# Unread matmuls in the pauses of a hand-ordered beginning, a later load of constants, and products moved ahead

## The chip, the cores and the metric

The kernel runs on one core of a Trainium2 chip. The metric is the time of the device for one execution, in microseconds (us), as the median of several runs. Beside these runs one execution is recorded by the hardware profiler: its span, from the first to the last instruction, and every instruction in it. The core's engines work side by side, each through its own instructions in order: TensorE (PE: matmuls; PEld: the loads of its stationary operand), VectorE (DVE), ScalarE (ACT), GpSimd (POOL) and SyncE (SP), which issues most DMA transfers here.

## The reference

A trunk of four residual layers over 256 tokens of 1024 features. Each layer has a token mixer (layer 0 and 3: sliding-window attention; 1: gated linear attention; 2: forgetting attention) and a SwiGLU network, each behind a norm that is shifted and scaled by vectors from the conditioning vector c. What matters for the change is the beginning of layer 0:

```
c_act = silu(c)
mod = c_act @ ada_w[0] + ada_b[0]              # 6 vectors of 1024
sh1, sc1, g1, sh2, sc2, g2 = split(mod, 6)
h = rmsnorm(x, gain) * (1 + sc1) + sh1
q, k, v = split(h @ w_in, ...)                 # 1024, 256 and 256 columns
q, k = rope(q), rope(k)                        # rotation by the position
...                                            # windowed softmax attention, output product
```

## The kernel before, in words

**Layout.** x is kept transposed: 8 tiles (KT) of 128 features by 256 tokens (S). Weights stream from memory in blocks of 1 MB, 128 partitions by 2048 columns of float32, which SP loads into one of five buffers `raw` (class `Stream`; a new load is issued when the block five before it is used up). A block of an ordinary weight is split into a high part `wh` (ACT, L195, a rounded copy) and a low part `wl` (DVE, L197, the rest), in two pieces of 1024 columns. There are three `wh`/`wl` pairs. Each product of float32 accuracy is then three matmuls of the faster format (`mm3`, L280 to L282): wh by hh, wl by hh, wh by hl, where hh and hl are the two parts of the activation h.

**The beginning** (`first_chunks`). Three kinds of blocks alternate in the stream, in the order of `ORDER0`: s and h are blocks of the scale and the shift vector of the first norm, w are blocks ("chunks") of the input projection. Chunk 0 holds the columns of the keys, chunk 1 those of the values; the next four give the queries.

1. ACT squares the 8 tiles of x, DVE adds the squares up, TensorE sums them over the partitions (`stat_start` L329, `stat_end` L342), ACT and DVE make 1/rms of it (`y`), TensorE spreads it over the partitions (L352), ACT copies it (`rbs`).
2. Four rounds follow. Round r uses one block s and one block h, which give two tiles each of scale and shift. A block is multiplied by c_act on TensorE (`ada_rows`, 16 matmul records at L231, "row products"), ACT copies the row that results (`fc`, L232), TensorE turns it into columns (L236, "turns": 4 records for a block, 8 for the two blocks of a round), and DVE adds the bias (L238). `h_tiles` then makes two tiles of h: DVE tk (L455), ACT hh (L457), DVE hl (L450). Between its two blocks a round does the products of chunk 0 with the tiles of the round before (`products`: 12 matmuls for two tiles). Behind rounds 0 and 2 the weights of chunk 0 and chunk 1 are split.
3. After the four rounds come the products that are left: chunk 1 with tiles 0 to 5, then both chunks with tiles 6 and 7.

`pinned` ties the instructions of `first_chunks` together, on each engine, in the order in which they are written. Everything else is put in order by the framework's scheduler, which may place other instructions between them.

**The second constants** (`const2`, 128 by 1024 of float32, 512 KB: the cosines and sines of the rotation, the masks of attention and more) are loaded by a DMA on ACT's queue, which stands behind round 1 in `first_chunks` (L809). The profile gives their tile and their source the same names as the first constants (const, in_const). The first to read them is the rotation of the keys (`rope`, L676 to L685, on DVE), which follows when chunk 0 is complete; then come the rotations of the queries (L676 to L683). TensorE turns the rotated keys (L701) and queries (L716) for attention, whose steps run beside the projections.

Of the kernel before, what the change touches and what calls it, by code (L numbers as in the profile page):

```python
# [20 lines left out]
S = 256  # L21
# [122 lines left out]
class Builder:  # L144
# [578 lines left out]
    def swa_heads(self, layer, pool, q_of, kT, v, oh, ol):  # L723
# [7 lines left out]
        def head(h):  # L731
            g, i = divmod(h, 4)
            rows = slice((i % 2) * HD, (i % 2 + 1) * HD)

            def pre():
                q = q_of(g)
                if g not in qTs and q is not None:
                    qTs[g] = self.swa_qT(pool, q)
                return q is not None
            return {  # L740
                "pre": pre, "ready": lambda: True,
                "q": lambda: qTs[g][rows, i // 2],
                "k": lambda: kT[0][rows, g],
                "v": lambda: [v[:, b, g * HD:(g + 1) * HD] for b in range(NB)],
                "sink": nsink[:, h:h + 1],
            }
        return self.attn_heads(pool, [head(h) for h in range(16)], self.c("masks")[:, :2 * P], oh, ol)

    def pinned(self, start):

        last = {}
        for ins in list(self.nc.cur_bb.bb.instructions)[start:]:
            if ins.engine in last:
                self.tc.add_manual_dep(
                    ins, last[ins.engine].name,
                    mybir.DependencyInfo(mybir.DependencyClass.NoSync, mybir.DependencyReason.DATA),
                    reason="first chunks")
            last[ins.engine] = ins

    def first_chunks(self):  # L760


        nc = self.nc
        start = len(nc.cur_bb.bb.instructions)
        self.A, self.late = None, []
        self.st.cap = self.st.widx[EARLY]
        self.per_tick = 0.0
        self.turns = []
        acc = None
        for k in range(KT):  # L770
            q = self.t(self.small, [P, S], "sq", bufs=4)
            nc.scalar.activation(q, self.x[:, k], AF.Square)
            if 0 < k < KT - 1:
                nc.vector.tensor_tensor(out=q, in0=acc, in1=q, op=ALU.add)
            acc, self.acc = q, acc
        self.last_sq = acc
        self.stat_start(self.acc)
        self.stat_end()
        rbs = self.t(self.small, [P, S], "rbs", bufs=1)
        nc.scalar.copy(rbs, self.spread(self.y))  # L780
        hs = hh, hl = self.h_alloc()
        A = self.t(self.small, [P, KT], "A", bufs=2)
        sh = self.mod[0][:, :KT]
        outs, ws, todo = [], [], []

        def products(n, chunks=slice(None)):
            for c, (wh, wl) in list(enumerate(ws))[chunks]:
                for k in range(todo[c], n):
                    for m in range(2):
                        sl = slice(m * P, (m + 1) * P)  # L790
                        self.mm3(outs[c][m][:, :S], hh[:, k, sl], hl[:, k, sl], wh[:, k], wl[:, k],
                                 k == 0, k == KT - 1)
                todo[c] = n
        for r in range(4):
            self.st.force_ada(0, (1,), r)
            products(2 * r, slice(1))
            self.st.force_ada(0, (0,), r)
            while self.turns:
                self.turns.pop(0)()
            self.mod_cols(0, 0, 2 * r, 2 * r + 2, A)  # L800
            self.h_tiles(range(2 * r, 2 * r + 2), rbs, A, sh, hh, hl)
            if r in (0, 2):
                c = len(ws)
                ws.append([x.rearrange("p (k n) -> p k n", k=KT) for x in self.st.get(f"i0_{c}")])
                self.st.cap = self.st.widx[EARLY]
                outs.append(self.banks(("mm", "s")[c])[0])
                todo.append(0)
            if r == 1:
                nc.scalar.dma_start(self.const2, self.a["const2"])  # L809
        products(KT - 2)  # L810
        products(KT)
        self.pinned(start)
        return hs, [[o[:, :S] for o in out] for out in outs]
# [649 lines left out]
```

## Time and profile before

| | |
|---|---|
| time, median of 3 runs | 1241.97 us (1241.35 to 1245.2) |
| time of the profiled execution | 1240.14 us |
| its span | 1238.4 us |
| mean granted TensorE clock | 0.997 |
| busy: PE, DVE, ACT, POOL | 97%, 80%, 57%, 10% of the span |
| DMA | 298.40 MB, mean 241 GB/s |

The profiled execution's time is its span and 1.7 us around it. Line numbers are those of the kernel before. In the profile, "mm" and "s" are the PSUM banks of chunk 0 and of chunk 1 in the beginning, "t" those of the row products, the turns and the sums. A float32 matmul of full accuracy shows as two records. In a list of waits or a timeline, "<-" behind the idle time names what ended it.

### The profile page before, as it was taken

The numbers are of one execution on the slowest core, as the hardware profiler recorded it, in microseconds if no ns is written. First come the engines' busy times: TensorE is split into PE (matmuls) and PEld (weight loads), VectorE is DVE, ScalarE is ACT, GpSimd is POOL, SyncE is SP. The second block draws the span as 40 slices with busy tenths as digits, with TensorE's granted clock in tenths as the row PEclk, the third lists the DMA queues.
The fourth block names the chain that finished last, engine by engine and source line by source line (L and its number), as shares of the span: only waits on it lengthen the run. The fifth ranks groups of instructions, "written<-read, shape, count | busy, mean of one in ns | idle before, by whom it ended". The sixth has DMA issues, their size and how long they took to land.

```text
span 1238.4 us, 19970 instructions
## 1 busy us (share of the span) xinstructions
PE 1207.4 (97%) x7540; PEld 1050.9 (85%) x7540; DVE 993.3 (80%) x1832; ACT 700.2 (57%) x1297; POOL 124.7 (10%) x173
## 2 busy tenths in 40 slices
PE   6999999999999999999999999999999999999997
PEld 4876988888988998888889999888889979888886
DVE  3888998889868799888877758988887998766553
ACT  4575744454676565444458777544445677544442
POOL 0020300001123111000121102100011011100011
PEclk9999999999999999999999999999999999999999
DMA  9956699889642248997875543889787534656440
GB/s 365 366 183 261 227 369 344 315 315 355 228 148 103 103 141 314 351 332 259 282 294 205 198 144 118 330 333 340 258 284 274 179 134 166 238 208 217 160 164 34
DMA packets 45106, 298.40 MB, mean 241 GB/s; under 512 B 5217, under 2 KB 5377, under 8 KB 14802
## 3 DMA queue, kind: packets, MB, share of 16 engines
q1 hardware_dynamic: 44210, 295.56, 65.6%
q8 instruction: 59, 0.97, 0.3%
q10 hardware_dynamic: 432, 1.05, 0.2%
q0 software_dynamic: 368, 0.53, 0.1%
q14 instruction: 37, 0.30, 0.1%
HBM read 296.03 MB, written 1.05 MB: 240 GB/s over the span
## 4 chain that ended last, share of the span: by engine, by line
PE 88%; DVE 5%; ACT 4%; issue 2%; POOL 0%; DMA 0%; DVEq 0%; SPq 0%; ACTq 0%; POOLq 0%
PE mm L1194 13%; PE mm L280 12%; PE mm L281 12%; PE mm L282 12%; PE s L282 7%; PE s L280 7%; PE s L281 7%; PE mm L1196 7%; PE s L613 2%; PE o L643 2%; PE t L1166 1%; PE t L654 1%; DVE wl L197 1%; ACT wh L195 1%; DVE x L551 1%
## 5 line engine op out<-in xcount | busy, mean ns | idle before, releaser
L197 DVE TENSOR_TENSOR wl<-raw,wh 128x1024 fp32r<-128x1024 f32 (+2 forms) x408 | 446.6, 1125 | 87.2 <-ACT wh L195 86.3
L195 ACT CAST wh<-raw 128x1024 fp32r<-128x1024 f32 (+2 forms) x408 | 376.8, 964 | 216.8 <-issue 91.7
L1194 PE MATMUL mm<-a,wh 128*128 128x512 f32 x704 | 247.9, 394 | 0.0
L214 DVE CUSTOM_DVE_ANT_0 raw<-raw,cact,const 128x1024 f32<-128x1024 f32 x168 | 214.1, 1290 | 4.7 <-DMA raw<-in_ada 4.5
L280 PE MATMUL mm<-wh,hh 128*128 128x512 f32 (+1 forms) x560 | 197.6, 353 | 2.0 <-ACT wh L195 1.1
L1196 PE MATMUL mm<-a,wl 128*128 128x256 f32 x704 | 196.6, 279 | 0.0
L281 PE MATMUL mm<-wl,hh 128*128 128x512 f32 (+1 forms) x560 | 193.4, 345 | 0.9 <-DVE wl L197 0.9
L282 PE MATMUL mm<-wh,hl 128*128 128x512 f32 (+1 forms) x560 | 193.8, 346 | 0.0
L1194 PEld LDWEIGHTS mm<-a,wh 128*128 128x128 f32 x704 | 131.9, 187 | 31.0
L280 PE MATMUL s<-wh,hh 128*128 128x512 f32 (+2 forms) x384 | 144.8, 378 | 1.5 <-ACT hh L457 1.5
L281 PE MATMUL s<-wl,hh 128*128 128x512 f32 (+2 forms) x384 | 142.6, 372 | 0.0
L282 PE MATMUL s<-wh,hl 128*128 128x512 f32 (+2 forms) x384 | 142.3, 374 | 0.0
L1196 PEld LDWEIGHTS mm<-a,wl 128*128 128x128 f32 x704 | 132.0, 187 | 0.2
L436 POOL TENSOR_TENSOR sq<-sq,sq 128x256 f32<-128x256 f32 x48 | 52.2, 1088 | 771.1 <-ACT sq L425 751.5
L280 PEld LDWEIGHTS mm<-wh,hh 128*128 128x128 f32 x560 | 106.1, 189 | 18.7 <-issue 3.5
L281 PEld LDWEIGHTS mm<-wl,hh 128*128 128x128 f32 x560 | 106.1, 190 | 13.9 <-DVE wl L197 1.1
L282 PEld LDWEIGHTS mm<-wh,hl 128*128 128x128 f32 x560 | 106.0, 189 | 13.8 <-issue 0.5
L551 DVE SCALAR_TENSOR_TENSOR x<-mm,mod,x 128x256 f32<-128x256 f32 x128 | 61.4, 479 | 40.2 <-PE mm L1196 32.2
L280 PEld LDWEIGHTS s<-wh,hh 128*128 128x128 f32 x384 | 72.2, 188 | 13.6 <-ACT hh L457 1.7
L282 PEld LDWEIGHTS s<-wh,hl 128*128 128x128 f32 x384 | 71.7, 188 | 13.3 <-DVE hl L450 0.2
L281 PEld LDWEIGHTS s<-wl,hh 128*128 128x128 f32 x384 | 72.3, 188 | 12.0
L280 PE MATMUL mm<-oh,wh 128*128 128x256 f32 x256 | 73.5, 292 | 1.7 <-DVE x L551 1.6
(228 smaller groups left out, 2009.5 us busy)
## 6 DMA issues: line engine op xcount, KB each, us to landing
raw<-in_ada SPq DMA_DIRECT2D x96, 1024.0 KB, 6.6
raw<-in_gu SPq DMA_DIRECT2D x88, 1024.0 KB, 6.5
raw<-in_down SPq DMA_DIRECT2D x64, 704.0 KB, 5.3
raw<-in_swa_in SPq DMA_DIRECT2D x12, 1024.0 KB, 5.9
raw<-in_gla_in SPq DMA_DIRECT2D x11, 1024.0 KB, 5.3
raw<-in_fox_in SPq DMA_DIRECT2D x11, 1024.0 KB, 4.9
raw<-in_swa_o SPq DMA_DIRECT2D x8, 1024.0 KB, 4.9
raw<-in_gla_o SPq DMA_DIRECT2D x4, 1024.0 KB, 4.9
```

Source lines behind the costliest of these rows:

```text
L195: nc.scalar.copy(wh[:, sl], raw[:, sl])
L197: eng.tensor_tensor(out=wl[:, sl], in0=raw[:, sl], in1=wh[:, sl].bitcast(F32), op=ALU.subtract)
L214: nc.vector.tensor_tensor_reduce(out=w, in0=w, in1=self.cact, scale=1.0, scalar=b, op0=ALU.mult, op1=ALU.add, accum_out=col)
L280: nc.tensor.matmul(out, ah, bh, start=first, stop=False)
L281: nc.tensor.matmul(out, ah, bl, start=False, stop=False)
L282: nc.tensor.matmul(out, al, bh, start=False, stop=last)
L436: (eng or nc.gpsimd).tensor_tensor(out=q, in0=self.acc, in1=q, op=ALU.add)
L551: self.nc.vector.scalar_tensor_tensor(out=self.x[:, m], in0=ps, scalar=gate[:, m:m + 1], in1=self.x[:, m], op0=ALU.mult, op1=ALU.add)
L613: nc.tensor.matmul(sc[:, so:s1], q[:, so:so + P], k[:, :k1], start=True, stop=True)
L643: nc.tensor.matmul(o[rows, b * P:S], vs[e][b], pt[:, e, :S] if b == 0 else pt[:, e, S:], start=b == 0, stop=b == 1)
L1194: nc.tensor.matmul(o, wh[:, k], a[:, kk].rearrange("p e n -> p (e n)"), start=kk == 0, stop=False)
L1196: nc.tensor.matmul(o[:, S:], wl[:, k], a[:, kk, 0], start=False, stop=kk == FT - 1)
```

## The change

- A new helper, `fill(n)`, issues n float32 matmuls of the identity with 256 columns of the first constants into a spare PSUM bank (tag "o", which attention's output uses later). Nobody reads their result. They are part of the pinned order of TensorE.
- Five of them stand ahead of the norm's sums, one behind the sums, one in each round between the second row product and the turns, and four, two and two at the end of rounds 0, 1 and 2, behind the issue of `h_tiles`.
- In round 3, chunk 1's products with tiles 0 to 3 (24 matmuls) stand ahead of the second row product. They were behind the turns. `todo` keeps the larger count, so that chunk 0 isn't done twice.
- The load of the second constants moves from the end of round 1 to the end of round 3.

```diff
+    def fill(self, n):
+        ident = self.c("ident")
+        for _ in range(n):
+            self.nc.tensor.matmul(self.spare[:, :S], ident, self.const[:, :S], start=True, stop=True)
...
         acc = None
+        self.spare = self.ps("o")
         for k in range(KT):
...
         self.last_sq = acc
+        self.fill(5)
         self.stat_start(self.acc)
         self.stat_end()
+        self.fill(1)
         rbs = self.t(self.small, [P, S], "rbs", bufs=1)
...
-                todo[c] = n
+                todo[c] = max(todo[c], n)
         for r in range(4):
             self.st.force_ada(0, (1,), r)
             products(2 * r, slice(1))
+            if r == 3:
+                products(4)
             self.st.force_ada(0, (0,), r)
+            self.fill(1)
             while self.turns:
                 self.turns.pop(0)()
             self.mod_cols(0, 0, 2 * r, 2 * r + 2, A)
             self.h_tiles(range(2 * r, 2 * r + 2), rbs, A, sh, hh, hl)
...
-            if r == 1:
+            if r < 3:
+                self.fill((4, 2, 2)[r])
+            else:
                 nc.scalar.dma_start(self.const2, self.a["const2"])
         products(KT - 2)
         products(KT)
```

## The prediction

> **What bounds the kernel now.** I read the page's busy shares and its chain first; then the table by stage (from:to, length, busy time of TensorE, its weight loads, DVE, ACT and POOL, granted clock, DMA share, GB/s), for the whole span and for the first 45 us; last the timelines of the first 60 us (start, length, engine, line, out<-in, and in brackets the idle time before with what ended it).
>
> ```profile
> span 1238.4 us, 19970 instructions
> PE 1207.4 (97%) x7540; PEld 1050.9 (85%) x7540; DVE 993.3 (80%) x1832; ACT 700.2 (57%) x1297; POOL 124.7 (10%) x173
> PE 88%; DVE 5%; ACT 4%; issue 2%; POOL 0%; DMA 0%; DVEq 0%; SPq 0%; ACTq 0%; POOLq 0%
> ...
> 0.00:31.00 31.00, 21.12 (x152) 12.81 (x152) 11.07 (x28) 12.99 (x26) 1.43 (x9) 0.94 0.92 364
> 155.00:186.00 31.00, 31.00 (x144) 25.53 (x143) 31.00 (x46) 13.76 (x19) 0.00 (x0) 1.00 0.98 370
> ```
>
> TensorE is busy in 97% of the span and carries 88% of the chain. A stage of the middle (last row) has no gap in it; the first 31 us have ten. So a microsecond that TensorE saves or loses in the beginning moves the end by about as much, and little else in the change can move it. The beginning has little to give: 0.3% of this kernel, about what a measurement of it can tell from no change, is 3.7 us.
>
> TensorE's timeline, and behind it four rows of the table by stage:
>
> ```profile
> 3.40 3.77 PE L1326 MATMUL mm<-hh,fc 1*128 1x512 f32 x4 [3.40 <-ACT hh L1321]
> 10.04 1.01 PE L329 MATMUL t<-const,sq 128*128 128x1 f32 x4 [2.86 <-DVE sq L774]
> 10.92 0.99 PE L342 MATMUL t<-const,sq 128*128 128x1 f32 x4
> 12.46 1.22 PE L352 MATMUL t<-const,y 128*128 128x128 f32 x4 [0.55 <-DVE y L346]
> 13.61 3.06 PE L231 MATMUL t<-raw,ccol 128*32 128x256 f32 x32
> 16.61 1.18 PE L236 MATMUL t<-const,fc 128*128 128x1 f32 x8
> 18.44 1.07 PE L231 MATMUL t<-raw,ccol 128*32 128x256 f32 x16 [0.66 <-DMA raw<-in_ada]
> 20.57 0.39 PE L280 MATMUL mm<-wh,hh 128*128 128x256 f32 x1 [1.06 <-ACT wh L195]
> 21.83 0.39 PE L281 MATMUL mm<-wl,hh 128*128 128x256 f32 x1 [0.87 <-DVE wl L197]
> ...
> 23.17 0.41 PE L281 MATMUL mm<-wl,hh 128*128 128x256 f32 x1
> 23.38 0.41 PE L282 MATMUL mm<-wh,hl 128*128 128x256 f32 x1
> 23.73 1.94 PE L231 MATMUL t<-raw,ccol 128*32 128x256 f32 x16
> 25.59 1.33 PE L236 MATMUL t<-const,fc 128*128 128x1 f32 x8
> ...
> 28.37 0.39 PE L280 MATMUL mm<-wh,hh 128*128 128x256 f32 x1 [0.45 <-ACT hh L457]
> ...
> 33.95 0.39 PE L280 MATMUL mm<-wh,hh 128*128 128x256 f32 x1 [0.45 <-ACT hh L457]
> ...
> 35.86 1.07 PE L231 MATMUL t<-raw,ccol 128*32 128x256 f32 x16
> 36.86 1.22 PE L236 MATMUL t<-const,fc 128*128 128x1 f32 x8
> ...
> 22.75:26.20 3.45, 3.45 (x25) 1.95 (x24) 0.16 (x1) 0.37 (x1) 0.00 (x0) 0.51 0.99 392
> 29.00:36.00 7.00, 6.52 (x66) 4.71 (x70) 3.12 (x9) 3.05 (x6) 0.00 (x0) 1.00 1.01 423
> 38.08:45.21 7.13, 7.13 (x61) 7.13 (x62) 5.77 (x13) 3.76 (x6) 0.00 (x0) 1.00 0.94 364
> ```
>
> Two things are to be seen. **The clock:** it is granted at 0.51 from 22.75 to 26.20, after pauses of 1.06 and 0.87 us, and the 16 row products (L231) take 1.94 there against 1.07 elsewhere. The start is slow as well, though no loss is recorded for it: the first 32 row products take 3.06, which is 1.94 + 1.07 within 0.05, so the clock rose half-way, near 15.6. **The pauses:** at 20.57 and 21.83 TensorE has waited for the split of the first weights (ACT, then DVE), at 28.37 and 33.95 for ACT's hh. From 35.86 to 45.21 it has none: its last 60 products take 7.13 us, 0.12 each.
>
> DMA doesn't bound these rounds. TensorE waits for it once, at 18.44, for the fourth block of 1 MB; the last vector block is six later and at 423 GB/s (2.5 us each) lands near 33.3, ahead of its use at 35.86.
>
> **The change, part by part.**
>
> *The price of a fill* (256 float32 columns): L1326 takes 3.77 for two products of 512 at the slow clock, so 0.94 for 256; half, 0.47, at the full one. (L231 gives 0.53: two turns of four side by side in 1.07.) The bank that the fills write is free until attention's output, so nobody waits but what stands behind them on TensorE.
>
> *fill(5)* starts at 7.17, when L1326 ends, and lasts 4.7 slow or 2.35 fast. The norm's sums, now at 10.04, come up to 1.8 us late, or no later. It gains if the clock rises sooner: sums from 1.9 to 1.0 (eight turns of the same shape take 1.2 at the full clock, now also those at 36.86), spread from 1.22 to 0.6, row products from 3.06 to 2.1. When does it rise? In the start it took 2.0 us of row products, or 5.6 from 10.04; in the recorded stretch 3.45. So 7.17 + 3.45 = 10.6 in the middle, 12.8 at the late end, and 9.0 at the early end, where L1326 counts too (3.40 + 5.6). Up at 9.0: fills end at 10.4, sums 11.4, y 0.55 later, spread 12.55, row products 14.7, a fill and the turns 16.35; they now end at 17.8, so 1.45 earlier. Up at 10.6 likewise 0.65 earlier; up at 12.8, 0.45 later. I take 0.5 earlier, the middle of the ends.
> The Trainium skill, TensorE: Matmul & The Clock Gate, Part 1, says that the clock rises after a busy window of about 3.4 us, and that these windows run freely. The trace agrees with its 3.45. By that rule the five fills alone would lift it between 10.6 and 14.0; at 14.0 the first turns would end 0.9 late and the beginning 1.4 later than now.
>
> *fill(1) behind the sums* lies in the 0.55 us wait for y: nothing.
>
> *fill(4), round 0*: 1.9 us from the turns' end at 17.3; the row products behind it end at 20.3, and the second product waits for wl until 21.83 - 0.5 = 21.33 anyway. Free. It fills the pauses after which the clock fell, so I take the slow stretch as gone: L231 0.87, turns 0.1, five products at 0.21 for 0.12 (0.45), together 1.4 us.
>
> *fill(1) ahead of the turns*: now the first turn of two covers ACT's copy of the second row; the fill pushes both: 0.47 on the path in each of the four rounds (round 0's stands above).
>
> *fill(2), rounds 1 and 2*: 0.94 where the pause is 0.45: 0.5 each on the path, against which the 12 products behind it no longer stumble (now 1.9 from 33.95 to 35.86 for what takes 1.44).
>
> *Along TensorE with these:* round 1's second row products end at 21.33 + 1.3 + 1.05 = 23.7 (now 25.7), its turns at 25.3; fill(2), row products and 12 products 28.75; row products, fill and turns 31.4; fill(2), row products, 12 products 34.85 (now 35.86).
>
> *Chunk 1 in round 3*: 24 of its products (2.9 us) move ahead of the last row products. They need the low part of chunk 1's weights from DVE. DVE's timeline, ACT's last hh, the present issue of the second constants, and a transpose that comes later:
>
> ```profile
> 35.27 2.36 DVE L197 TENSOR_TENSOR wl<-raw,wh 128x1024 fp32r<-128x1024 f32 x2 [0.45 <-ACT wh L195]
> 39.25 1.22 DVE L197 TENSOR_TENSOR wl<-raw,wh 128x1024 fp32r<-128x1024 f32 x1
> 43.61 0.42 DVE L676 TENSOR_TENSOR r<-mm,const 128x256 f32<-128x256 f32 x1 [1.21 <-PE mm L282]
> 45.67 1.21 DVE L197 TENSOR_TENSOR wl<-raw,wh 128x1024 fp32r<-128x1024 f32 x1
> 46.81 0.68 DVE L685 TENSOR_TENSOR ul<-r,r 128x512 f32<-128x512 f32 x1
> 47.41 3.48 DVE L197 TENSOR_TENSOR wl<-raw,wh 128x1024 fp32r<-128x1024 f32 x3
> 51.17 0.42 DVE L676 TENSOR_TENSOR r<-mm,const 128x256 f32<-128x256 f32 x1 [0.28 <-PE mm L282]
> 54.17 0.42 DVE L683 TENSOR_TENSOR qr<-r,r 128x256 f32<-128x256 f32 x1
> ...
> 38.97 0.91 ACT L457 ACTIVATE hh<-tk,mod 128x256 fp32r<-128x256 f32 x2 [0.23 <-DVE tk L455]
> ...
> 28.21 0.39 ACTq L809 DMA_DIRECT2D const<-in_const  x1
> ...
> 57.28 0.66 PE L716 MATMUL t<-const,qr 128*128 128x128 f32 x4
> ```
>
> The first half of that wl is done at 36.45, with the round 1.05 earlier at 35.4: a wait of 0.5 that the present order doesn't have. The move fills no pause, since there is none from 35.86 on; and the 12 products of chunk 1 that stay behind the turns (1.44) just cover the 1.45 us from turns to hh (26.92 to 28.37). So: 35.4 + 2.8 = 38.2, row products 39.2, fill 39.7, turns 40.85, 36 products 45.15; now 45.21. **Sum of the beginning: 0.05 earlier, even**; 1.0 earlier with the clock up at 9.0, 0.9 later at 12.8.
>
> *The second constants*: DMA queues, with the issue, its size and time to landing, then the constants' queue alone from 31 to 32 and from 32 to 33 us (packets, MB, share):
>
> ```profile
> const<-in_const ACTq DMA_DIRECT2D x1, 512.0 KB, 7.9
> const<-in_const SPq DMA_DIRECT2D x1, 221.5 KB, 2.7
> ...
> q10 hardware_dynamic: 13, 0.05, 12.9%
> ...
> q10 hardware_dynamic: 44, 0.18, 43.7%
> ```
>
> Leaving the middle of the loads (1.25 us at 423 GB/s) gains nothing, since TensorE waits for no DMA after 18.44. The issue moves behind ACT's last hh: now that would be at 39.4; the turns end at 40.85 for 38.08, so 42.2. With 7.9 us they land at 50.1, with the 2.7 of the lightly loaded start at 44.9. The keys' rotation (L676, which reads them) could start when chunk 0 ends, at 43.7; its transfer was hidden and is now 1.2 to 6.4 us late. I take 7.9: the queue is as full there (DMA share 0.94 against 1.01).
> The Trainium skill, DMA: Bandwidth & Descriptors, Queues, rings and completion order, says that an engine takes turns between its queues packet by packet. The 43.7% agree. By that rule 0.5 MB at half the rate would take 2.5 us behind the 3 us before the first packet, and land near 47.7.
>
> The cost depends on what stands behind the rotation on DVE, which works in order. The next weights' wl (45.67) is needed when TensorE has done 48 products after 45.15: 50.9. If it is placed ahead of the rotation, as the wl at 39.25 stands between steps of the last round, it is done by 47.3, and the rotations of keys (2.7) and queries (3.4, 51.17 to 54.59) by 56.2, ahead of the transpose at 57.28: nothing. If it stays behind: 50.1 + 2.06 + 1.2 = 53.4, TensorE waits 2.5, and the transpose behind DVE's later work about 1 more: 3.5. I take nothing, since the wl would be ready while the constants are not, and keep 3.5.
>
> **Sum against the profiled execution** (span 1238.4, time 1240.14): 0.05 less, 1240.1. The median shown, 1241.97, lies 1.8 above that execution: 1241.9, and with some small wait 1242.0. Even.
>
> **The rivals.**
> (a) *Slower: DVE stands at the second constants.* Place: L676, ready at 43.7. It decides if they land after 47.6 (50.9 less 2.06 and 1.2) and wl is behind. Price 2.5 to 3.5, with a late clock up to 4.5: 1245.3. For it: 7.9 us, and today's order, rotation first. Against: wl stood early at 39.25.
> (b) *Faster: the clock is full from 7 to 9 us on*, and the runs that weren't recorded, 1.8 above the recorded one, lose more to it today. 1.0 by the sum, and 1.7 (half of 3.45) for one more slow stretch avoided: 1239.2. For it: L1326 and the fills are 8 us without a pause. Against: 0.47 a fill, on the path in four rounds.
> (c) *The fills don't lift the clock.* Then 1.8 for fill(5), 0.94 and three times 0.47 for the fills ahead of the turns, about 0.5 for the rest: 4.7, so 1246.7. Against: the row products, float32 as well, lifted it near 15.6.
>
> **How the numbers follow.** Even 0.58 (own range 1240.4 to 1243.8: 1.0 and 0.9 on either side, and 0.7 for waits that I don't see); (a) 0.23; (b) 0.14; (c) 0.05. More than 0.3% is below 1238.2 or above 1245.7. Faster: half of (b) and a little of even, 0.09. Slower: a third of (a), most of (c), 0.11. Within: 0.80. The range reaches to about the middles of (b) and (a): 1239.0 to 1245.5.
>
> **What would show it.** Right: granted clock 1.00 from 20 to 30 us and 1.07 for row products in every round; 0.43 to 0.53 a fill; turns half a microsecond behind the row products; a short wait for wl before chunk 1's first products; the end of chunk 1 between 44 and 46.3; wl ahead of L676 on DVE. (a) would show as over 4 us idle before L676 and TensorE waiting for wl near 51; (c) as 1.94 for the row products of rounds 0 and 1. The whole would be wrong if the steps of attention behind 60 us came in another order than now, which I take as unchanged.

## The result, and the profile after

The change makes the kernel slower: 1250.66 us as the median of 9 runs (1247.1 to 1253.3), against 1242.46 of the kernel before in 9 runs beside them (1241.35 to 1246.0). The ratio is 1.0052, 95% interval 1.0039 to 1.0065; the ratios given here are those on record for all runs of both kernels, not quotients of the two medians. The forecast was 1242.0, and the time lies above its range. The profiled execution of after took 1251.17 us, 11.03 more than that of before; their spans are 1249.4 and 1238.4.

The page of after, its first lines and the head of the chain of work that ended last:

```profile
span 1249.4 us, 20036 instructions
PE 1219.8 (98%) x7576; PEld 1060.4 (85%) x7576; DVE 994.0 (80%) x1832; ACT 700.8 (56%) x1297; POOL 124.1 (10%) x173
...
PE 87%; DVE 6%; ACT 3%; issue 2%; DMA 1%; POOL 0%; DVEq 0%; SPq 0%; ACTq 0%; POOLq 0%
```

The page alone would mislead: TensorE's share of the span went up, to 98%. What changed in the chain is small and telling: DMA, at 0% before, has 1%, and DVE 6% for 5%.

TensorE's timeline of after, first the beginning, then the rows behind it that have a wait:

```profile
3.81 2.08 PE L753 MATMUL o<-const 128*128 128x256 f32 x4 [3.81 <-DMA const<-in_const]
5.82 3.78 PE L1340 MATMUL mm<-hh,fc 1*128 1x512 f32 x4
9.53 2.93 PE L753 MATMUL o<-const 128*128 128x256 f32 x6
12.25 0.56 PE L329 MATMUL t<-const,sq 128*128 128x1 f32 x4
...
14.45 1.93 PE L231 MATMUL t<-raw,ccol 128*32 128x256 f32 x32
...
16.85 0.95 PE L236 MATMUL t<-const,fc 128*128 128x1 f32 x8
17.66 1.97 PE L753 MATMUL o<-const 128*128 128x256 f32 x8
19.56 1.07 PE L231 MATMUL t<-raw,ccol 128*32 128x256 f32 x16
...
38.83 1.07 PE L231 MATMUL t<-raw,ccol 128*32 128x256 f32 x16
39.83 0.70 PE L753 MATMUL o<-const 128*128 128x256 f32 x2
...
52.43 0.36 PE L280 MATMUL mm<-wh,hh 128*128 128x256 f32 x1 [0.95 <-DVE r L679]
54.80 0.39 PE L281 MATMUL mm<-wl,hh 128*128 128x256 f32 x1 [0.59 <-DVE wl L197]
...
61.01 0.55 PE L716 MATMUL t<-const,qr 128*128 128x128 f32 x3 [0.55 <-DVE qr L683]
98.24 0.45 PE L716 MATMUL t<-const,qr 128*128 128x128 f32 x1 [2.80 <-DVE qr L683]
```

A fill (two records) is 1.0 us at the slow clock (2.93 for three) and 0.49 at the full one (1.97 for four). The sums start at 12.25, 2.2 later than before, but take 0.56 for 1.01, and the 32 row products 1.93 for 3.06: the clock rose near 12.4. The first turns end at 17.8, as before. Every later group of 16 row products takes 1.07. So the beginning of this execution came out even, as forecast. By the end of chunk 1 this text means the moment when 96 products of the input projection have been issued, 48 for either chunk: 45.57; it was 45.21. (Where the 24 products are moved, the scheduler puts twelve products of the next chunk ahead of chunk 1's last twelve, which start only then.) Four waits follow, each for something that VectorE makes; of these the kernel before had only the last, 0.76 us long.

VectorE's timeline of after, and the issue of the second constants on ScalarE's queue:

```profile
40.98 1.22 DVE L197 TENSOR_TENSOR wl<-raw,wh 128x1024 fp32r<-128x1024 f32 x1
...
46.85 1.23 DVE L197 TENSOR_TENSOR wl<-raw,wh 128x1024 fp32r<-128x1024 f32 x1 [2.53 <-ACT wh L195]
51.47 0.42 DVE L676 TENSOR_TENSOR r<-mm,const 128x256 f32<-128x256 f32 x1 [3.39 <-DMA const<-in_const]
...
53.53 1.22 DVE L197 TENSOR_TENSOR wl<-raw,wh 128x1024 fp32r<-128x1024 f32 x1
...
43.29 0.38 ACTq L823 DMA_DIRECT2D const<-in_const  x1
```

The load is issued at 43.29 and its reader starts at 51.47, 8.2 later. One piece of wl stands ahead of the rotation, the next (53.53) behind it. VectorE idles 2.53 and 3.39 us, and the first rotation starts 5.9 us behind the end of chunk 1; before, it started 1.6 ahead of it.

One line tells the rest. It is the table by stage for the stretch from the end of chunk 1 to the start of the first residual add (L551), in which both kernels issue the same products; first of before, then of after:

```profile
45.21:96.20 50.99, 50.20 (x384) 40.61 (x384) 46.13 (x136) 36.36 (x96) 8.34 (x24) 1.00 0.66 241
```

```profile
45.57:103.81 58.24, 53.06 (x382) 41.77 (x380) 47.57 (x140) 37.70 (x97) 7.47 (x24) 0.95 0.58 212
...
96.00:100.00 4.00, 1.76 (x4) 0.65 (x5) 4.00 (x12) 3.03 (x5) 0.98 (x3) 0.71 0.90 307
100.00:104.00 4.00, 4.00 (x15) 2.19 (x13) 1.48 (x6) 0.97 (x2) 0.00 (x0) 0.50 0.26 107
350.00:354.00 4.00, 4.00 (x24) 4.00 (x23) 0.30 (x1) 1.68 (x3) 0.00 (x0) 0.57 0.75 268
388.00:392.00 4.00, 4.00 (x22) 3.72 (x21) 2.90 (x5) 1.85 (x3) 0.00 (x0) 0.59 0.20 31
```

Of the 11.0 us between the two spans, 0.4 is the end of chunk 1 and 7.2 is this stretch (58.24 for 50.99). Of the 7.2, 4.4 is idle time of TensorE (5.18 for 0.79: length less busy time) and 2.9 is longer busy time, most of it at a lower clock: around the pause of 2.80 the clock falls, and it is granted at 0.50 behind it (second and third row). To the ninth residual add another 0.65 us is lost, and 2.9 in the second layer, where TensorE waits as before but has two stretches of a low clock (the last two rows). Why the clock falls there isn't settled, but it isn't a mark of this change's loss: the kernel with the load at round 2 (below), whose VectorE doesn't wait for the constants, has 0.57 from 344 to 348 and from 382 to 386 us in its profiled execution and loses 2.8 us there as well. The nine runs of after reflect that last part: those with a mean clock of 0.997 took 1247.1 to 1249.2, those with 0.993 to 0.995 took 1249.5 to 1253.3.

### The profile page after: what moved, and what is told of

The parts are those of the page before. It is cut to its first block, busy times and chain, and to the rows that moved or that the text cites. A ratio compares the mean times of both kernels' runs of the same rounds, so it can differ in the third digit from the quotient of the medians.

```text
span 1249.4 us, 20036 instructions
## 1 busy us (share of the span) xinstructions
PE 1219.8 (98%) x7576; PEld 1060.4 (85%) x7576; DVE 994.0 (80%) x1832; ACT 700.8 (56%) x1297; POOL 124.1 (10%) x173
## 4 chain that ended last, share of the span: by engine, by line
PE 87%; DVE 6%; ACT 3%; issue 2%; DMA 1%; POOL 0%; DVEq 0%; SPq 0%; ACTq 0%; POOLq 0%
PE mm L1208 13%; PE mm L280 12%; PE mm L281 11%; PE mm L282 11%; PE s L282 7%; PE s L280 7%; PE s L281 7%; PE mm L1210 7%; PE s L613 2%; PE o L643 2%; DVE wl L197 2%; PE t L1180 1%; PE t L654 1%; ACT wh L195 1%; DMA const<-in_const 1%
## 5 line engine op out<-in xcount | busy, mean ns | idle before, releaser
L551 DVE SCALAR_TENSOR_TENSOR x<-mm,mod,x 128x256 f32<-128x256 f32 x128 | 61.5, 480 | 41.3 <-PE mm L1210 33.4
```

The source lines that it names most:

```text
L551: self.nc.vector.scalar_tensor_tensor(out=self.x[:, m], in0=ps, scalar=gate[:, m:m + 1], in1=self.x[:, m], op0=ALU.mult, op1=ALU.add)
```

## The experiments

The theory after the first look: the late constants make VectorE stand at the keys' rotation, and it is this stand that costs, not the fills. The rivals: the fills cost TensorE time; the moved products cost by themselves; the late load costs by itself; and, inside the theory, only one consequence of the stand counts (the wl behind the rotation, or the PSUM bank that the rotation still reads). Ratios are against the kernel before, run beside each experiment; its medians there were 1245.79, 1245.39, 1244.92 and 1242.18 us. Some executions of kernels without fills have a low clock through much of the beginning, as shown at the end, so single microseconds are compared within the traces, from the end of chunk 1 on.

**One part undone, or one part alone.** The load back at the end of round 1:

```diff
-            else:
+            if r == 1:
                 nc.scalar.dma_start(self.const2, self.a["const2"])
```

> The changed kernel with the load of the second constants back behind round 1; fills and the chunk 1 products stay. Theory (the late load: DVE waits for it at the keys' rotation, TensorE then for a PSUM bank, for wl and for the queries, and a slow clock follows): nearly the whole loss goes, 1241.5 to 1244 us, no idle time over 1.3 us before the first L676, chunk 1 done near 46. Rival 1 (the fills): stays at 1248 or above. Rival 2 (the products moved ahead of the last row product): stays at 1248 or above.

Measured: 1243.39 us (1242.95 to 1245.37), ratio 0.999 [0.9978, 1.0003].

Only the load moved (kernel before, `if r == 3:` in place of `if r == 1:`):

> The kernel before with the load of the second constants alone moved behind round 3. Theory (the late load): slower by 5 to 9 us, 1247 to 1251; the load lands some 8 us after its issue near 39.5, so near 47.5, and DVE waits for a DMA before L676. Rivals 1 and 2: within 1.5 us of the kernel before. If the late load costs only because the beginning has also grown longer by the other two parts, it is slower by 1 to 4.

Measured: 1244.27 us (1241.42 to 1248.16), 1.0002 [0.9987, 1.0018]. The theory's 1247 to 1251 is missed. VectorE waited 5.72 us for the constants, and it cost the stretch behind chunk 1 only 1.5 us (52.5 for 51.0, table below).

Only the fills (the load at the end of round 1, chunk 1 not moved):

> The kernel before with the fills alone (5, 1, one a round, 4, 2, 2). Theory (the late load): within 1.5 us of the kernel before, granted clock 1.00 from 20 to 30 us. Rival 1 (the fills cost): slower by 4 us or more.

Measured: 1242.09 us (1241.54 to 1244.68), 0.9979 [0.9968, 0.999].

Only the moved products:

```diff
             products(2 * r, slice(1))
+            if r == 3:
+                products(4)
```

> The kernel before with chunk 1's first 24 products alone moved ahead of the last row product. Theory (the late load): 0.5 to 1.5 us slower, by a wait for wl of some 0.5 and by the last steps of the round coming 3 us later on DVE and ACT. Rival 2 (the moved products carry the loss): slower by 4 us or more.

Measured: 1244.89 us (1241.64 to 1247.81), 1.0001 [0.9989, 1.0014].

No part is slow by itself; the fills gain 0.2%. So two parts must meet. The pairs that were left:

> The changed kernel without the products moved ahead: fills and the late load. Theory (the moved products bring the last hh, and with it the issue, some 3 us nearer to the end of chunk 1, so that the load lands behind the point at which TensorE needs DVE's next work): 1 to 3 us above the fills alone, 1243 to 1245.5. Rival (fills and late load together carry the loss, the moved products have no part): 1248 or above.

Measured, fills and late load: 1242.21 us (1240.13 to 1243.66), 0.9978 [0.9966, 0.999]: nothing above the fills alone, where 1 to 3 us were expected.

> The kernel before with the moved products and the late load, without fills. Theory (the late load costs where the products have been moved ahead of its issue, whatever the fills): 3 to 8 us slower than the kernel before, 1246 to 1251, with a wait of DVE for a DMA before L676 and TensorE waiting behind it. Rival (it takes all three parts): within 1.5 us of the kernel before.

Measured, moved products and late load: 1250.64 us (1249.49 to 1254.37), 1.0059 [1.0037, 1.008].

That is the whole loss, without a fill in the kernel. What the two do together is a matter of distance: the issue stands behind the last hh, and the 24 moved products (2.9 us) are taken from behind that hh and put ahead of it. In the kernel with the load alone the issue is 5.8 us ahead of the end of chunk 1 (45.81 to 51.64), in after 2.3 (43.29 to 45.57).

**The stand taken away.** Layer 0's rotations read the first 256 columns of the first constants in place of the cosines and sines (other numbers, the same instructions), and so don't wait; the load stays late:

```diff
-        cos = self.c("cos")...
-        sin = self.c("sin")...
+        tabs = [self.const[:, :128], self.const[:, 128:256]] if self.layer == 0 else [self.c("cos"), self.c("sin")]
```

> The changed kernel whose rotations of layer 0 read 256 columns of the first constants in place of the cosines and sines (other numbers, the same instructions), so that the late load stays but nobody waits for it before attention's masks. Theory (the wait of the rotation on DVE carries the loss): near the changed kernel with the load put back, 1242.5 to 1245 us, no wait for a DMA before L676. Rival (the late load costs by taking its share of the loads of weights near 45 us): stays at 1248 or above.

Measured: 1241.36 us (1240.41 to 1244.07), 0.9979 [0.9967, 0.999]: all of the loss is gone, and the gain of the fills is left. VectorE's first rotation in this kernel, and the stretch from the end of chunk 1 to the first residual add:

```profile
45.57 0.42 DVE L676 TENSOR_TENSOR r<-mm,const 128x256 f32<-128x256 f32 x1 [1.09 <-PE mm L282]
```

```profile
45.73:97.00 51.27, 49.99 (x384) 40.56 (x384) 47.42 (x141) 37.41 (x97) 6.42 (x24) 1.00 0.64 240
```

The load one round earlier, `if r == 2:` in place of `else:`, removes the stand without other numbers:

> The changed kernel with the load behind round 2, not 3. Issued near 33 and landing 8 us later near 41, ahead of the end of chunk 0 near 45. Theory (only a landing behind the end of chunk 0 costs): 1242.5 to 1245. Rival (any load later than round 1 costs in proportion, by the loads that it delays): between 1245 and 1249.

Measured: 1243.38 us (1240.74 to 1245.57), 0.9987 [0.9975, 0.9998]; no wait for the constants.

**Which consequence of the stand?** In after one piece of wl stands behind the rotation, and the bank that the rotation reads keeps TensorE from the next chunk (0.95 us at 52.43). First the whole wl of that chunk ahead of the rotation:

```diff
+            self.st.cap = self.st.widx[3]
+            self.st.force(self.st.pos["i0_3"])
```

> The changed kernel with the split of the second query weights (both pieces of wl) written ahead of the keys' rotation, so that DVE has done it before it waits for the late load. By the prediction's step (wl ahead of the rotation: nothing) the loss goes, 1242 to 1244. Theory now (TensorE also waits for the bank of chunk 0, which only the rotation frees, and the rotations of the queries come late): half of it stays, 1245 to 1248.

Measured: 1249.95 us (1247.3 to 1252.91), 1.0048 [1.0031, 1.0066], above what either theory had. Then also the bank set free, by a copy of chunk 0's results that the rotation reads:

```diff
+            for ap in early[0]:
+                parts.append(self.t(self.small, [P, S], "fc", bufs=2))
+                nc.scalar.copy(parts[-1], ap)
```

> As the kernel with wl ahead, and chunk 0's two results copied by ACT from PSUM to SBUF, where the rotation reads them, so that its banks are free at once. If the bank is the rest of the loss: 1241.5 to 1244. If the late rotations themselves carry it (the transposes of keys and queries on TensorE, attention behind them): as the kernel with wl ahead, 1245 to 1248.

Measured: 1248.52 us (1242.45 to 1251.1), 1.0029 [1.0011, 1.0047]. TensorE's waits in this last kernel from 45 to 110 us (us in total, times, longest):

```profile
PE t L716 <- ACT wh L195: 2.8, 1, 2.8
PE t L716 <- DVE qr L683: 1.8, 2, 1.4
```

Neither the bank nor a wl is waited for in this stretch, and by the two ratios (1.0029 of 1.0052, with intervals that overlap) more than half of the loss is still there. The two waits for VectorE are at 60.91 and 62.76 us, at the first transposes of the rotated queries (L716). The one of 2.8 is at 99.64, at the last of them; the profile puts it down to ScalarE's split of a weight, and the kernel without the stand waits 1.27 for VectorE at the same place. What carries it was not separated.

**How long may VectorE stand?** In the kernel with fills and late load it stood 5.6 us and nothing was lost; the kernel with moved products and late load lost some 7 us. To separate "free up to about 3 us behind the end of chunk 1" from "costs from the first microsecond", the load of after was issued one step earlier:

```diff
             self.st.force_ada(0, (0,), r)
+            if r == 3:
+                nc.scalar.dma_start(self.const2, self.a["const2"])
             self.fill(1)
```

> The changed kernel with the load of the second constants issued one step earlier on ScalarE's queue: in round 3 between the second row product and the turns, ahead of the last hh, not behind it. In the changed kernel the second row's copy on ScalarE ends near 40.2 us and the issue stands at 43.29, so this issue comes near 40.5 and with 8.1 us lands near 48.6; the first rotation then starts about 3 us behind the end of chunk 1 (5.9 in the changed kernel; a moved load alone had 2.9, fills and load 2.8). Theory 1, a late rotation costs nothing up to some 3 us behind the end of chunk 1 and about as much as it is later from there on: VectorE idles near 3 us for the constants, TensorE waits under 0.5 us for wl and for the bank, the first residual add comes 51 to 52.5 us behind the end of chunk 1 (58.2 in the changed kernel), and the time is 1241.5 to 1243.5. Theory 2, each microsecond that VectorE stands there costs its share of the loss: (3.0 + 0.2) / (5.9 + 0.2) of some 7.5 us, so 1246 to 1247.5.

Measured: 1245.98 us (1243.76 to 1249.33), 1.002 [1.0006, 1.0035]: just under what theory 2 forecast, and well above theory 1, which falls. Its first rotation, TensorE's waits for VectorE from 30 to 105 us, and the stretch:

```profile
50.92 0.42 DVE L676 TENSOR_TENSOR r<-mm,const 128x256 f32<-128x256 f32 x1 [4.42 <-DMA const<-in_const]
```

```profile
PE t L716 <- DVE qr L683: 1.7, 2, 1.3
PE s L613 <- DVE nm L626: 0.6, 1, 0.6
PE mm L281 <- DVE wl L197: 0.5, 1, 0.5
...
```

```profile
47.74:101.80 54.06, 51.22 (x384) 40.98 (x384) 47.32 (x140) 37.62 (x97) 6.41 (x24) 1.00 0.62 228
```

This kernel, the one with the load back at round 1 and the one without the stand have the same instructions in the same order on VectorE and, but for two neighbours, on TensorE. So the comparison is clean: a rotation that starts 3.2 us behind the end of chunk 1, not 0.2 ahead of it, makes the stretch 2.8 us longer (54.06 for 51.27), at a full clock throughout. That is 0.8 us for each microsecond. The reason stands in the first 20 us of the stretch, here without the stand, then with the load half back:

```profile
45.73:65.73 20.00, 20.00 (x165) 18.81 (x164) 19.38 (x52) 14.63 (x29) 0.65 (x5) 1.00 0.78 299
47.74:67.74 20.00, 18.44 (x142) 16.43 (x141) 16.82 (x40) 12.37 (x19) 0.02 (x1) 1.00 0.71 264
```

Without the stand VectorE has 19.4 us of work in these 20 us, and TensorE has no gap. With it TensorE falls behind, matmul by matmul against the kernel without the stand, by 0.6 us at 54.26 (a wl), 1.6 at 61.60 (the transposes of the queries) and 2.7 at 66.64 (the first products of queries with keys, L613), and it stays 2.7 to 2.8 behind to the end of the stretch; at the last transposes both wait 1.27. VectorE's reserve (47.4 us of work in 51.3, 92%) lies behind these 20 us. It is no help there, since in the next 20 us TensorE itself is busy for 20.00.

In the kernel with fills and late load the framework's scheduler put the steps of attention in another order than in the one just shown. VectorE's rotation starts 2.8 us behind the end of chunk 1 there, and the stretch is 51.07:

```profile
47.39:98.46 51.07, 49.11 (x384) 40.28 (x384) 47.21 (x141) 35.94 (x96) 6.91 (x24) 1.00 0.67 248
```

TensorE loses as much in the first 20 us there (busy for 18.34), but in the last 11 it idles 0.3 us, where the kernel without the stand idles 1.3, and the 384 matmuls take 49.1 us for 50.0. That the order of the steps makes the difference between this kernel and the one above is argued from the two orders; a run of the one order with the other's load wasn't made. The table puts the kernels together (us):

| kernel | issue ahead of the end of chunk 1 | first rotation against it | from there to the first residual add | ratio |
|---|---|---|---|---|
| before | 17.0 | -1.6 | 51.0 | 1 |
| load back at round 1 | 18.4 | -0.2 | 51.2 | 0.999 |
| load at round 2 | 12.4 | -0.2 | 51.3 | 0.9987 |
| no stand | 2.3 | -0.2 | 51.3 | 0.9979 |
| fills and late load | 5.9 | 2.8 | 51.1 | 0.9978 |
| seven early fills, late load (below) | 5.8 | 3.9 | 52.2 | 0.9972 |
| late load alone | 5.8 | 2.9 | 52.5 | 1.0002 |
| load half back | 5.5 | 3.2 | 54.1 | 1.002 |
| wl ahead | 2.3 | 5.5 | 56.2 | 1.0048 |
| moved products and load | 2.3 | 5.5 | 57.4 | 1.0059 |
| wl ahead, bank free | 2.3 | 5.9 | 56.0 | 1.0029 |
| after | 2.3 | 5.9 | 58.2 | 1.0052 |

**Better fills.** Two tries to get the clock up sooner. First, kernel before with two early fills on a tile of ones (it needs no load), then three on the constants, one behind the sums, four in round 0:

> The kernel before with fewer fills, placed where they cover pauses: two from about 1.3 us on that read a tile of ones, three ahead of the norm's sums, one behind them, four in round 0; none ahead of the turns, none in rounds 1 and 2; load and products as before. If the fills help by raising the clock early and hurt by 0.47 us each where they stand on the path: clock up at 5 to 9 us, sums near 10, 1.5 to 2.5 us below the fills alone, 1239.5 to 1241. If it is the many fills of all rounds that keep the clock up: as the kernel before, with slow stretches from 20 to 35 us in some executions, 1242 to 1246.

Measured: 1243.35 us (1241.48 to 1245.41), 0.9989 [0.9979, 1.0]; the first forecast is missed, and the clock rose no sooner (shown at the end). Then seven fills without a gap from 1.1 us on, the spread of c (a product of one row) moved behind them, and the load late:

```diff
+        warm = self.t(self.small, [P, S], "tk", bufs=3)
+        nc.gpsimd.memset(warm, 1.0)
+        self.fill(7, warm)
...
+        for i, ps in enumerate(cps):
+            nc.tensor.matmul(ps, one, crow[:, i * 512:(i + 1) * 512], start=True, stop=True)
```

> The kernel before with the late load (free without the moved products), seven fills without a pause from about 1.2 us on that read a tile of ones, the product that spreads c moved behind them, one fill behind the norm's sums, four in round 0, no others. The row-wide product doesn't count for the clock in the runs so far, and a window needs to be nearly full of matmuls; seven fills cover 6.6 us, two windows of 3.4, so the clock rises by 8.3 at the latest, the sums start near 10, and nothing stands ahead of the turns: 1 to 3 us below the fills alone, 1239 to 1241. Rival (the loads of 1 MB bound the four rounds once TensorE is faster): within 0.7 us of the fills alone, 1241.5 to 1242.5.

Measured: 1240.59 us (1239.43 to 1243.01), 0.9972 [0.996, 0.9984], the lowest median of all that was run. It waited 1.20 us for a wl at 51.45. With its load back at the end of round 1:

> The kernel with the contiguous early matmuls (seven on a tile of ones from 1.1 us, the products with c behind them, one behind the sums, four at the end of round 0, chunk 1 not moved), with the load of the second constants where it was before the change, at the end of round 1. The one with the late load took 1240.59 and waited 1.20 us for wl at 51.45 us. By the theory that this wait is all that its late load cost: no wait there, the first rotation ahead of the end of chunk 1 and the first residual add 51.0 us behind it (52.2 with the late load), time 1239.0 to 1240.2. By the rival that the load takes its share of the queue from the weights when it stands in the middle of the rounds: 1240.6 or more, with TensorE waiting for a block of weights or of vectors between 25 and 45 us.

Measured: 1241.53 us (1239.54 to 1243.3), 0.9988 [0.9974, 1.0001]. The wait for wl is gone and the stretch behind chunk 1 is 51.0, as the first theory has it; but chunk 1 ends at 45.52, not at 44.22, so the time is the rival's. TensorE pauses 0.95 us at 32.02 ahead of round 3's first row products, where the kernel with the late load paused 0.32, and the clock is granted at 0.72 from 32 to 38. That the load in the middle of the rounds delays a block is likely, not shown: the trace names VectorE's tk as what ended the pause. The two ratios overlap.

## Why the prediction was wrong, point by point

**The beginning: right for the profiled execution, and there partly by luck.** The forecast had it 0.05 earlier, with 1.0 to either side; it is 0.36 later. The fills cost what was said (0.49 at the full clock), the slow stretch at 22.75 is gone, the wait for wl ahead of chunk 1 was 0.34 (0.5 taken); the first turns ended when they did before (0.5 earlier was taken). But the prediction let the five fills run together from 7.17. In after two run ahead of the product that spreads c (3.81) and three behind it (9.53), 2.08 and 2.93 us of them. The clock rose at 12.4, near the late end of what the prediction allowed (12.8). Nine profiled kernels have these five fills, and only after and the one without the stand had it up by then: their first 32 row products take 1.93. In the other seven these take 2.43 to 3.48, so the clock rose only within them (the traces' own record of the clock has 16.7 to 18.95 us), and chunk 1 ended at 47.1 to 48.4. With the fills alone:

```profile
9.65 2.93 PE L753 MATMUL o<-const 128*128 128x256 f32 x6
12.37 0.85 PE L329 MATMUL t<-const,sq 128*128 128x1 f32 x4
...
15.92 2.56 PE L231 MATMUL t<-raw,ccol 128*32 128x256 f32 x32
```

By the 3.4 us windows that the Trainium skill (TensorE: Matmul & The Clock Gate, Part 1) names, the prediction estimated that the five fills would lift it between 10.6 and 14.0. The 12.4 of after agrees, the other seven do not.

**The load: nearly right.** Issue at 43.29 for 42.2, of which 0.7 comes from a wl (40.98, above) that slipped between VectorE's two bias additions ahead of the last hh. It took 8.2 us, where 7.9 were taken. The 5.5 us that the prediction worked out beside it from the Trainium skill (DMA: Bandwidth & Descriptors, Queues, rings and completion order) was too short. The constants' queue in after, from 47 to 48, from 48 to 49 and from 49 to 50 us (packets, MB, share), had a third of the time at first, and near the half of that estimate only in the last of the three:

```profile
q10 hardware_dynamic: 34, 0.14, 33.8%
...
q10 hardware_dynamic: 35, 0.14, 34.8%
...
q10 hardware_dynamic: 58, 0.19, 47.3%
```

**The step that failed** is the cost of the late constants: "I take nothing, since the wl would be ready while the constants are not, and keep 3.5." In its place the profiled execution lost 7.2 us behind the end of chunk 1, and where the rotation doesn't wait the loss is gone (0.9979). Three things are wrong with the step.
- The framework's scheduler put only one of the two pieces ahead of the rotation. But the experiment with the whole wl ahead has 1.0048: had the guess been right, the forecast would have failed as well. It also missed that the rotation holds chunk 0's bank, worth 0.95 at 52.43.
- It asked whether single results would be ready in time, and not how much VectorE has to do meanwhile. The test that was missing is one row of the kernel before, the 20 us behind the end of chunk 1:

```profile
45.21:65.21 20.00, 19.98 (x163) 18.59 (x162) 19.22 (x50) 13.37 (x28) 0.65 (x5) 1.00 0.78 298
```

  VectorE has 19.2 us of work there and TensorE no gap, so a stand of several microseconds has no room. The prediction quoted DVE at 80% of the whole span and asked only about queues behind the rotation. It also ended at the first readers. For the transposes that it compared (57.28, with rotations done by 56.2) TensorE waited only 0.55; the 2.80 came at 98.24, at the last of four groups of transposes. VectorE was still behind there: its last wl ahead of them starts 49.9 us behind the end of chunk 1, and 44.7 in the kernel before. (Not all of that wait is the stand's: TensorE waits 0.76 at this place in the kernel before and 1.27 in the one without the stand. Part may be DMA's: with VectorE late the five buffers stay full, nothing is loaded from 80 to 84 us, and ScalarE waits 0.6 us for weights near 97. How much, was not separated.)
- A pause of TensorE cost more than its length: of the 7.2, up to 2.9 are the low clock around the 2.80. The forecast had no term for it; rival (a) had 1.0.

**The rivals.** (a) named the place and the mechanism, with the right start (TensorE held up at 51 to 54 us) and half of the price: 1.5 us there for 2.5, but 7.2 over the whole stretch for 3.5 (4.5 with a late clock). Of its two conditions the first, landing after 47.6, was met by 2.5 us in the forecast's own numbers; 0.23 for the other was too little. (b) has the fills' gain right and its reason half: the clock was up at 7 to 9 us in none of the nine kernels with these fills. But other executions do lose more without them. Of the four profiled kernels without fills, two (before, moved products alone) had the clock up near 16 us, and two (late load alone, moved products and load) only at 36, with chunk 1 ending at 51.6 to 51.7. With the fills alone the runs lie close together (1241.54 to 1244.68, where the kernel before beside them has 1240.71 to 1248.44), and the ratio is 0.9979; the loss hides it. (c) holds in part: in seven of the nine the fills ahead of the sums didn't lift the clock. Its slow rounds 0 and 1 didn't come, since the row products of round 0 lifted it, as its own objection says.

## What to carry to other kernels

When a load moves later, find its first reader, then ask how busy that reader's engine is in the stretch right behind it, before the engine that sets the time next has a gap: here VectorE had 19.2 us of work in the first 20, and a reserve further on was no help. Parts of a change that are each free can share one reserve: here the late load and the moved products both lived on the 6 us between the issue and the end of chunk 1. The unread matmuls in the pauses did pay, 0.2 to 0.3%, and it was the other two parts that took it back.

## What the runs showed of the hardware

TensorE's timeline of the kernel with the load moved alone, and its table by stage for the same time:

```profile
19.34 1.93 PE L231 MATMUL t<-raw,ccol 128*32 128x256 f32 x16
...
29.76 1.93 PE L231 MATMUL t<-raw,ccol 128*32 128x256 f32 x16
...
37.36 1.07 PE L231 MATMUL t<-raw,ccol 128*32 128x256 f32 x16
```

```profile
16.00:36.00 20.00, 18.40 (x120) 11.69 (x112) 6.66 (x16) 5.42 (x11) 0.00 (x0) 1.00 0.94 360
```

The row products take 1.93 for 1.07, so the clock was at half until about 36 us, yet the column of the granted clock has 1.00. In these traces a clock that has not been raised yet isn't recorded as low: in the beginning the durations tell it, not the column.

What raises it is seen in the two kernels with early fills, first the one with gaps, then the one without:

```profile
1.11 2.07 PE L752 MATMUL o<-tk 128*128 128x256 f32 x4 [1.11 <-POOL tk L1332]
4.36 2.93 PE L752 MATMUL o<-const 128*128 128x256 f32 x6 [1.17 <-DMA const<-in_const]
7.21 3.78 PE L1339 MATMUL mm<-hh,fc 1*128 1x512 f32 x4
13.69 1.01 PE L329 MATMUL t<-const,sq 128*128 128x1 f32 x4 [2.70 <-DVE sq L779]
```

```profile
1.11 5.69 PE L751 MATMUL o<-tk 128*128 128x256 f32 x14 [1.11 <-POOL tk L1336]
6.73 1.98 PE L784 MATMUL mm<-hh,fc 1*128 1x512 f32 x4
10.23 1.01 PE L329 MATMUL t<-const,sq 128*128 128x1 f32 x4 [1.52 <-DVE sq L778]
```

With gaps, 8.7 us of matmuls ahead of 11 us didn't raise the clock (sums still at 1.01), though the last 6.6 of them were contiguous; 3.78 of these are the product that reads one partition. Without gaps 14 records took 5.69 where the slow clock would need 6.9 (0.98 for two), so the clock rose within them, and had fallen again by 10.23 (1.01 for the sums), behind the product of one row and a pause of 1.52. In the seven kernels with five fills whose clock rose late, two fills, this product and three fills stand without a gap for 8.6 us (from 3.6 or later to 12.2 or later), and didn't raise it either. The simplest reading is that the product of one row doesn't count as work for the clock; no run took that product by itself.
